# Merge gates of a hybrid decoder layer moved to the front and formed by seven half-size products

## The chip, the cores and the metric

One core of a Trainium2 chip runs the whole layer as one program. The metric is the device time of that core in microseconds. The engines in the text: PE is the tensor engine (its weight loads are PEld), DVE the vector engine, ACT the scalar engine, POOL is GpSimd, SP issues most transfers. A product is one matmul instruction with a 128x128 stationary part and 512 moving columns.

## The reference

One layer on 512 tokens with 2048 features, in float32:

```python
h = _rms_norm(x, norm_g[i])
proj = jnp.einsum("bld,dn->bln", h, w_in[i])
(z_ssd, xbc, dt, u_pool, z_pool, q, k, v, z_attn, gate_logits) = jnp.split(proj, IN_SPLITS, axis=-1)
y_ssd = _ssd_branch(z_ssd, xbc, dt, ...)
y_pool = _pool_branch(u_pool, z_pool, ...)
y_attn = _attn_branch(q, k, v, z_attn, ...)
gates = jax.nn.sigmoid(gate_logits.reshape(b, seq, N_BRANCHES, D_MODEL))
merged = (gates[:, :, 0] * (y_ssd @ w_br_ssd[i])
          + gates[:, :, 1] * (y_pool @ w_br_pool[i])
          + gates[:, :, 2] * (y_attn @ w_br_attn[i]))
x = x + merged @ w_out[i]
ple_gate = jax.nn.sigmoid(_rms_norm(x, ple_norm_g[i]) @ w_ple_gate[i])
x = x + ple_gate * (p[i] @ w_ple_proj[i])
```

The gate logits are h (512 x 2048) times 6144 columns of w_in, 2048 for each branch. y_ssd and y_pool have 2048 features, y_attn 512.

## The kernel before

Everything on PE is fed by one weight stream. `plan` lists entries of 512 KB; for each, `load` (L93) issues a transfer on SP into one of three `raw` buffers, and `split` (L101) makes two float32r parts of it: `hi` by a cast on ACT (L116), `lo` by a subtraction on DVE (L117; on POOL for entries 2 to 5). There are three `hi` and three `lo` buffers, so the cast of an entry waits until PE is through with the entry three before it. A job asks for the split two entries ahead of the one that it multiplies, and `split` asks for the load three further. Each pair of blocks takes three products: hi x hi, hi x lo, lo x hi (`product`, L124). So an entry has 24 products. `job_a` (L129) is token-major: 256 rows by 512 columns of weights move, the activations stand, and four PSUM banks fill at once. `job_b` (L157) is feature-major: the weights stand (512 rows by 256 columns), the tokens move, and two banks fill.

Activations are kept the same way: Hh and Hl are the two parts of the normed input, feature-major (128 features x 512 tokens, 16 of them). Small steps of the branches stand in two queues, `tasks` and `other`; `tick` (L74) runs one step of each after each entry, and `flush` runs them all. All four engines work in the order in which the program names their instructions. Short-lived tiles, 128x512, come from one pool `tp` of 52; transposes and small products use three PSUM banks (`PS`), the jobs five (`PG`).

The order of the jobs: the embedding's projection (kept in DRAM as ple_d, with the transposes of x beside it, `x_turn`), attention q, k, v, Z_ATT, SSD's dt and xbc, its z, then three merges. A merge (L910) alternates `gate_job`, whose two banks go through a sigmoid on ACT to SBUF (L894), with `br_job`, whose banks are multiplied by the gate on DVE (L903) and added to m on POOL (L907). Two gate jobs stand ahead of each first branch job, and m comes out feature-major, as the output projection needs it. `y_norm`, `ya_split` and `yp_split` make the branch's two parts as tasks beside these gate jobs, `m_split` those of m. The pooling jobs stand between the attention merge and the last; `pooled` (L953) runs beside its Z_POOL jobs.

Of the kernel before, what the change touches and what calls it, by code (L numbers as in the profile page):

```python
# [9 lines left out]
F32 = mybir.dt.float32  # L10
# [16 lines left out]
# groups 1 and 2 work on blocks of every 4th token (a block of group 2 holds 4 of its 16 strides)  # L27
# [4 lines left out]
def hybrid_kernel(ctx: ExitStack, tc: tile.TileContext, x, p, norm_g, w_in, conv_w, conv_b, dt_bias, a_log,  # L32
# [11 lines left out]
    tp = ctx.enter_context(tc.tile_pool(name="tp", bufs=NT))  # L44
    wp = ctx.enter_context(tc.tile_pool(name="wp", bufs=3))
    psum = ctx.enter_context(tc.tile_pool(name="psum", bufs=3, space=PSUM))
    dram = ctx.enter_context(tc.tile_pool(name="dram", bufs=1, space=DRAM))
    ctx.enter_context(tc.manual_schedule())

    def T(name="t", dtype=F32):  # L50
        return tp.tile([128, L], dtype, name=name, tag="t")
# [41 lines left out]
    def load(n):  # L93
        while state["dma"] <= n and state["dma"] < len(plan):
            src, k, c = plan[state["dma"]]
            t = wp.tile([128, k, c], F32, name="raw", tag="raw", bufs=3)
            nc.sync.dma_start(out=t, in_=src.rearrange("(k p) c -> p k c", p=128))
            raws[state["dma"]] = t
            state["dma"] += 1

    def split(n):  # L101
        while state["split"] <= n and state["split"] < len(plan):
            i = state["split"]
            load(i)
            r = raws.pop(i)
            _, k, c = plan[i]
            if c == 32:
                # the narrow entry keeps its two parts side by side
# [4 lines left out]
            else:  # L113
# [4 lines left out]
                parts[i] = (hi, lo)  # L118
            state["split"] += 1
# [9 lines left out]
    def job_a(w, c0, kn, xk, evac, pre=None, post=None):  # L129
        """Token-major [128 tokens, 512 columns]; xk(kt, t) gives the activations' two parts."""  # L130
# [26 lines left out]
    def job_b(w, c0, kn, xk, evac, pre=None, post=None, tiles=2):  # L157
        """Feature-major [128 features, 512 tokens]; xk(kt) gives the activations' two parts."""
# [46 lines left out]
    def rsqrt(dst, src, tmp, inv_n):  # L205
        """dst = 1 / sqrt(src * inv_n + EPS), with one Newton step behind the table."""
# [38 lines left out]
    def load_columns():  # L245
# [6 lines left out]
        # d_skip of the head that a feature belongs to  # L252
# [21 lines left out]
    def warm(n):  # L274
        """Products that nobody reads keep the tensor engine's clock up until the first weights are in."""
        ps = PG()
        for _ in range(n):
            PE.matmul(ps[:, 0:128], lhsT=ident, rhs=ident, start=True, stop=True)

    def start():  # L280
# [9 lines left out]
        def g_rows(j):  # L290
            # the selected row of norm_g on every partition
# [84 lines left out]
    hook(flush)  # L376
    hook(lambda: tasks.append(load_columns()))

# [4 lines left out]
    def make_masks():  # L383
# [3 lines left out]
        # keys of the block before: k >= q; of the same block: k <= q  # L387
# [6 lines left out]
        # every 16th token: within a block of every 4th, the keys whose place is the query's modulo 4  # L394
# [146 lines left out]
    zs_att, Ya = {}, {}  # L541

    def za_evac(j):
        def f(n, ps):
            z = T("za")
            A.activation(z, ps, AF.Silu)
            zs_att[2 * j + n] = z
# [4 lines left out]
    def combine():  # L552
# [34 lines left out]
        for h in range(4):  # L587
# [11 lines left out]
            V.tensor_mul(o, o, zs_att[h])  # L599
            Ya[h] = o  # L600

    for j in range(2):
        job_b(w_in, Z_ATT + j * 256, 16, hk, za_evac(j))

# [41 lines left out]
    def dt_task(o):  # L646
# [19 lines left out]
        # softplus(v) = max(v, 0) + log1p(e), e = exp(-|v|); log1p(e) = 2 atanh(e / (2 + e))  # L666
# [54 lines left out]
    def load_bc(n):  # L721
        """The rows of cumulated log decays of chunk n % 4 and the heads of group n // 4, on every partition."""
        while bc_at["n"] <= min(n, 15):
# [5 lines left out]
            if c > 0:  # L729
                # the growth since the chunk's start: even heads on partitions 0-63, odd ones on 64-127  # L730
# [155 lines left out]
    hook(lambda: tasks.append(y_norm()))  # L886

# [1 line left out]
    m, gs, done = {}, {}, {i: 0 for i in range(16)}  # L889

    def gate_job(br, f):
        def ev(n, ps):
            g = T("g")
            A.activation(g, ps, AF.Sigmoid)  # L894
            gs[2 * f + n] = g
        job_b(w_in, GATES + br * D + f * 256, 16, hk, ev)

    def br_job(w, kn, xk, f, first, pre=None):
        def ev(n, ps):
            i = 2 * f + n  # L900
            done[i] += 1
            g = gs.pop(i)
            V.tensor_mul(g, g, ps)  # L903
            if first:
                m[i] = g
            else:
                G.tensor_tensor(m[i], m[i], g, op=ALU.add)  # L907
        job_b(w, f * 256, kn, xk, ev, pre=pre)

    def merge(br, w, kn, xk, first, pre=None, after_gates=None):  # L910
        gate_job(br, 0)
        for f in range(8):
            if f < 7:
                gate_job(br, f + 1)
# [204 lines left out]
```

## Time and profile before

| what | us |
|---|---|
| median of the two runs | 2709.87 |
| the runs | 2712.01 and 2707.73 |
| span of the profiled execution | 2707.0 |
| median above that span | 2.9 |

The page counts busy time of each engine over the span and follows the chain of work that ended last. The profiled execution has no time of its own beside its span; the two runs lie 0.7 and 5.0 us above it. PE rows overlap: a product's row lasts about 0.39 us, while the next starts 0.23 us later, so the pitch is read from starts, not from durations. A row "out<-in" names the tile written and the tiles read; "[4.38 <-PE pg L126]" behind it is the idle time before it and what ended that.

### The profile page before, as it was taken

What the parts mean: (1) busy time and instruction counts of PE and PEld (TensorE: products, weight loads), DVE (VectorE), ACT (ScalarE), POOL (GpSimd) and SP (SyncE); (2) the same over time, 40 slices, a digit from 0 to 9 for tenths busy, and PEclk for the clock granted to TensorE, in tenths of its full rate; (3) what the DMA queues carried; (4) which work ended last, traced back from release to release, by engine and by line L of the source; (5) the groups of instructions that cost most, each with busy time, mean ns of one, the idle gap of its engine ahead of it and who ended that gap; (6) DMA issues with size and microseconds to landing.
All of it is one profiled execution on the core that took longest, in us unless ns stands there. A gap on an engine that the chain in (4) does not pass through costs nothing.

```text
span 2707.0 us, 29886 instructions
## 1 busy us (share of the span) xinstructions
PE 2689.0 (99%) x12310; PEld 2236.5 (83%) x12310; DVE 1098.3 (41%) x1456; ACT 840.0 (31%) x1133; POOL 208.7 (8%) x198
## 2 busy tenths in 40 slices
PE   8999999999999999999999999999999999999999
PEld 6888989888788888888888888888888888888887
DVE  6334333346776655322223333334442222433333
ACT  4233333443444434222222222222242222322322
POOL 5000000001211113000000110000000000000000
PEclk9999999999999999999999999999999999999999
DMA  7422323234644423333333333333333333333343
GB/s 227 100 88 77 94 78 94 77 93 105 168 118 127 113 86 86 109 94 101 94 101 93 101 94 98 97 94 101 87 108 93 101 94 97 113 114 119 112 153 101
DMA packets 238672, 284.56 MB, mean 105 GB/s; under 512 B 12620, under 2 KB 187528, under 8 KB 238536
## 3 DMA queue, kind: packets, MB, share of 16 engines
q1 hardware_dynamic: 236968, 278.74, 34.6%
q0 software_dynamic: 1568, 3.92, 1.0%
q8 instruction: 96, 1.57, 0.2%
q14 instruction: 40, 0.33, 0.0%
HBM read 274.08 MB, written 8.54 MB: 104 GB/s over the span
## 4 chain that ended last, share of the span: by engine, by line
PE 96%; DVE 2%; DMA 1%; ACT 1%; issue 0%; SPq 0%; DVEq 0%; ACTq 0%
PE pg L125 31%; PE pg L126 31%; PE pg L127 31%; PE ps L802 1%; PE ps L490 0%; PE ps L458 0%; PE ps L421 0%; DVE cv L614 0%; PE ps L785 0%; DVE x L326 0%; PE ps L791 0%; DVE ple L365 0%; PE ps L1044 0%; PE ps L477 0%; DVE lo L117 0%
## 5 line engine op out<-in xcount | busy, mean ns | idle before, releaser
L117 DVE TENSOR_TENSOR lo<-raw,hi 128x1024 fp32r<-128x1024 f32 x464 | 585.2, 1262 | 1221.7 <-ACT hi L116 1219.2
L116 ACT CAST hi<-raw 128x1024 fp32r<-128x1024 f32 x468 | 490.5, 1051 | 1153.7 <-PE pg L126 820.3
L125 PE MATMUL pg<-hh,hi 128*128 128x512 f32 x1984 | 782.7, 394 | 0.0
L127 PE MATMUL pg<-hh,lo 128*128 128x512 f32 x1984 | 772.5, 389 | 0.0
L126 PE MATMUL pg<-hl,hi 128*128 128x512 f32 x1984 | 772.4, 389 | 0.0
L125 PEld LDWEIGHTS pg<-hh,hi 128*128 128x128 f32 x1984 | 372.6, 188 | 81.2 <-issue 3.9
L126 PEld LDWEIGHTS pg<-hl,hi 128*128 128x128 f32 x1984 | 372.7, 188 | 78.4 <-issue 3.1
L127 PEld LDWEIGHTS pg<-hh,lo 128*128 128x128 f32 x1984 | 372.5, 188 | 78.0
L125 PE MATMUL pg<-hi,hh 128*128 128x512 f32 x576 | 230.0, 399 | 0.0
L127 PE MATMUL pg<-hi,hl 128*128 128x512 f32 x576 | 225.8, 392 | 0.0
L126 PE MATMUL pg<-lo,hh 128*128 128x512 f32 x576 | 225.7, 392 | 0.0
L127 PEld LDWEIGHTS pg<-hi,hl 128*128 128x128 f32 x576 | 124.2, 216 | 17.8
L125 PEld LDWEIGHTS pg<-hi,hh 128*128 128x128 f32 x576 | 124.4, 216 | 16.5
L126 PEld LDWEIGHTS pg<-lo,hh 128*128 128x128 f32 x576 | 124.4, 216 | 16.4
L907 POOL TENSOR_TENSOR g<-g 128x512 f32<-128x512 f32 x32 | 41.9, 1308 | 1216.7 <-DVE g L903 1192.3
L125 PE MATMUL pg<-hi,mh 128*128 128x512 f32 x256 | 100.1, 391 | 0.0
L125 PE MATMUL pg<-hi,xh 128*128 128x512 f32 x256 | 99.8, 390 | 0.0
L127 PE MATMUL pg<-hi,ml 128*128 128x512 f32 x256 | 99.7, 389 | 0.0
L126 PE MATMUL pg<-lo,mh 128*128 128x512 f32 x256 | 99.6, 389 | 0.0
L127 PE MATMUL pg<-hi,xl 128*128 128x512 f32 x256 | 99.6, 389 | 0.0
L126 PE MATMUL pg<-lo,xh 128*128 128x512 f32 x256 | 99.6, 389 | 0.0
L125 PE MATMUL pg<-yh,hi 128*128 128x512 f32 x256 | 99.6, 389 | 0.0
(289 smaller groups left out, 2722.2 us busy)
## 6 DMA issues: line engine op xcount, KB each, us to landing
raw<-in_w_in_dram SPq DMA_DIRECT2D x320, 512.0 KB, 3.6
raw<-in_w_br_ssd_dram SPq DMA_DIRECT2D x32, 512.0 KB, 3.5
raw<-in_w_br_pool_dram SPq DMA_DIRECT2D x32, 512.0 KB, 3.5
raw<-in_w_out_dram SPq DMA_DIRECT2D x32, 512.0 KB, 3.6
raw<-in_w_ple_gate_dram SPq DMA_DIRECT2D x32, 512.0 KB, 3.6
bc<-acT_d SPq DMA_DIRECT2D x32, 256.0 KB, 4.7
x<-in_x_dram SPq DMA_DIRECT2D x16, 256.0 KB, 6.8
ple_d<-ple SPq DMA_DIRECT2D x16, 256.0 KB, 2.8
```

The lines of the kernel that those rows point to most:

```text
L116: A.copy(hi, r)
L117: (G if 1 < i < EARLY else V).tensor_tensor(lo, r, hi.bitcast(F32), op=ALU.subtract)
L125: PE.matmul(ps, lhsT=lh, rhs=rh, start=first, stop=False)
L126: PE.matmul(ps, lhsT=lh, rhs=rl, start=False, stop=False)
L127: PE.matmul(ps, lhsT=ll, rhs=rh, start=False, stop=last)
L802: PE.matmul(pd[q, rows(h // 2)], lhsT=xdt[:, h * 64:h * 64 + 64], rhs=bc[h // 4][:, rows(h % 4)], start=True, stop=True)
L907: G.tensor_tensor(m[i], m[i], g, op=ALU.add)
```

## The change

The gates of all three branches are formed first, right after the embedding's projection, and stored in DRAM (gate_d). They are made in six blocks of 1024 columns by Strassen's method in Winograd's form: h is cut in two halves of tokens and two of features (L11, L12, L21, L22), the weights in two of rows and two of columns (a, b over c, d). Four sums S1 to S4 of h's quarters are made once (`make_left`), and four T1 to T4 of the weights' for each entry (T2 = d - b + a, T3 = d - b, T1 = d - T2, T4 = T2 - c). The seven products are L11 a, S2 T2, S3 T3 in a first pass, S4 d, S1 T1 in a second, L12 c, L22 T4 in a third; d is loaded twice. Each entry has 12 products. The results are summed on DVE in `st` tiles, go through a sigmoid on ACT and are stored by ACT's own transfers. While this runs, the pool of 52 tiles is closed and its room holds the sums (`swap`).

The branch products become token-major (`job_a`) and read their gates from DRAM, four tiles of 128x512 at a time; m is token-major and is turned by transposes (`m_turn`). The Z_ATT jobs move behind SSD's z, its result and the attention's go through DRAM (za_d, ya_d), and the attention merge moves into the first pooling group, behind its U_POOL jobs. `PS` has two banks, `PG` six. The cut diff:

```diff
-        return psum.tile([128, L], F32, name="ps", tag="s", bufs=3)
+        return psum.tile([128, L], F32, name="ps", tag="s", bufs=2)
-        return psum.tile([128, L], F32, name="pg", tag="g", bufs=5)
+        return psum.tile([128, L], F32, name="pg", tag="g", bufs=6)
...
     def split(n):
         while state["split"] <= n and state["split"] < len(plan):
             i = state["split"]
+            if callable(plan[i]) and "sp" not in held:
+                return
             load(i)
-            r = raws.pop(i)
-            _, k, c = plan[i]
+            if callable(plan[i]):
+                r, k, c = plan[i]("raw"), 2, L
...
+    def make_left():
...
+        for q0 in (0, 4):
+            x = {}
+            for n in ("L11", "L21", "L22", "L12"):
+                x[n] = sp.tile([128, 4, 256], F32, name="x4", tag="t2", bufs=4)
+                (G if n == "L12" else V).tensor_tensor(x[n], part(0, n), part(1, n), op=ALU.add)
+            x["S3"] = sp.tile([128, 4, 256], F32, name="x4", tag="rs", bufs=2)
+            V.tensor_sub(x["S3"], x["L11"], x["L21"])
+            V.tensor_add(x["L22"], x["L21"], x["L22"])
+            V.tensor_sub(x["L11"], x["L22"], x["L11"])
+            V.tensor_sub(x["L12"], x["L12"], x["L11"])
+            for n, o in (("S2", "L11"), ("S3", "S3"), ("S4", "L12"), ("S1", "L22")):
+                h, l = (SC[n][i][:, q0:q0 + 4] for i in range(2))
+                A.copy(h, x[o])
+                V.tensor_sub(l, x[o], h.bitcast(F32))
+            yield
...
+        passes.append([(entry("a", e, (("a", False),)), entry("T2", e, (("b", True), ("d", False))),
+                        entry("T3", e, ())) for e in range(4)])
+        passes.append([(entry("d", e, (("d", False),)), entry("T1", e, ())) for e in range(4)])
+        passes.append([(entry("c", e, (("c", False),)), entry("T4", e, ())) for e in range(4)])
+        lefts = (("L11", "S2", "S3"), ("S4", "S1"), ("L12", "L22"))
...
+                elif name == "S1":
+                    o = tile_()
+                    V.tensor_add(st["u2", t], st["u2", t], p)
+                    V.tensor_add(o, st["u3", t], p)
+                    evac(t, 1, st["u2", t], st["u2", t])
+                    evac(2 + t, 1, o, o)
+                elif name == "L12":
+                    evac(t, 0, p, tile_())
+                elif name == "L22":
+                    V.tensor_sub(st["u3", t], st["u3", t], p)
+                    evac(2 + t, 0, st["u3", t], st["u3", t])
...
+    def gate_evac(br, j):
+        def f(t, half, src, o):
+            A.activation(o, src, AF.Sigmoid)
+            c = (j + half) * L
+            nc.scalar.dma_start(out=gate_d[br, rows(t), c:c + L], in_=o)
+        return f
+
+    def enter():
+        swap("sp")
+        load(state["split"])
+        split(state["split"])
+        tasks.append(make_left())
+        step(tasks)
+
+    hook(enter)
+    for br in (0, 2, 1):
+        for j in (0, 2):
+            s_block(GATES + br * D + j * L, gate_evac(br, j))
+    hook(lambda: swap("tp"))
...
+        for j in range(4):
+            job_a(w, j * L, kn, lambda kt, t: tuple(a[:, rows(t)] for a in xk(kt)), ev(j),
+                  pre=lambda j=j: (pre() if pre and j == 0 else None, load_gates(br, j)),
+                  post=(lambda j=j: after(j)) if after else None)
...
+    def m_turn(j):
...
+        yield
+        for k in range(4):
+            kt = 4 * j + k
+            ps = PS()
+            for t in range(4):
+                PE.transpose(ps[:, rows(t)], m[t, j][:, rows(k)], ident)
+            A.copy(MT["h"][:, kt], ps)
+            V.tensor_sub(MT["l"][:, kt], ps, MT["h"][:, kt].bitcast(F32))
+            if k % 2:
+                yield
+
+    merge(1, w_br_pool, 16, lambda kt: Yph[kt], False, pre=flush, after=lambda j: tasks.append(m_turn(j)))
+    hook(lambda: [step(tasks) for _ in range(2)])
```

The instructions at three places. First DVE where the normed input is complete; hl is its second part, turned by `x_turn`. Before:

```order
L336 TENSOR_TENSOR hl_99<-pg_552,hh_98 128x4x128
L396 TENSOR_REDUCE mask_559<-ident_74 128x4
L397 TENSOR_SCALAR mask_559<-mask_559 128x4
L399 TENSOR_TENSOR mask_559<-mask_559 128x128
L117 TENSOR_TENSOR lo_580<-raw_351,hi_579 128x1024
```

After that, only the masks stand ahead of the next weight entry's lo.

The same place on DVE in the changed kernel; the x4 tiles are quarter sums of h, t2 is T2, rs holds b and then T3 (the last hl and two more L239 rows stand just ahead):

```order
L239 TENSOR_TENSOR x4_578<-hh_98,hl_99 128x1024
L241 TENSOR_TENSOR x4_582<-x4_574,x4_576 128x1024
L242 TENSOR_TENSOR x4_578<-x4_576,x4_578 128x1024
L243 TENSOR_TENSOR x4_574<-x4_578,x4_574 128x1024
L244 TENSOR_TENSOR x4_580<-x4_580,x4_574 128x1024
L248 TENSOR_TENSOR S2l_569<-x4_574,S2h_568 128x1024
L248 TENSOR_TENSOR S3l_571<-x4_582,S3h_570 128x1024
L248 TENSOR_TENSOR S4l_573<-x4_580,S4h_572 128x1024
L248 TENSOR_TENSOR S1l_567<-x4_578,S1h_566 128x1024
L274 TENSOR_TENSOR rs_560<-raw_562,rs_560 128x1024
L276 TENSOR_TENSOR t2_596<-rs_560,raw_554 128x1024
L137 TENSOR_TENSOR lo_607<-rs_560,hi_606 128x1024
```

The first half of `make_left`, eleven rows, has come in between hl and the first T2 and T3; its second half follows the last row shown, and the masks stand behind the gates.

Second, SP at the same place. Before:

```order
L97 DMA raw_447<-in_w_in_dram 128x2x512
L368 DMA ple_d_81<-ple_491 128x512
L368 DMA ple_d_81<-ple_494 128x512
L368 DMA ple_d_81<-ple_497 128x512
L368 DMA ple_d_81<-ple_500 128x512
L97 DMA raw_577<-in_w_in_dram 128x2x512
```

The last four stores of the embedding's projection are shown; a load of w_in stands ahead of each such four. In the changed kernel, from the last store but one:

```order
L536 DMA ple_d_81<-ple_488 128x512
L536 DMA ple_d_81<-ple_491 128x512
L264 DMA raw_554<-in_w_in_dram 128x2x512
L264 DMA rs_560<-in_w_in_dram 128x2x512
L264 DMA raw_562<-in_w_in_dram 128x2x512
L264 DMA raw_564<-in_w_in_dram 128x2x512
```

All sixteen stores now stand ahead of the first load of w_in.

Third, ACT where gates leave PSUM; hi is the cast of a weight entry. Before, at the start of the last merge:

```order
L116 CAST hi_13790<-raw_13686 128x1024
L894 ACTIVATE g_13820<-pg_13688 128x512
L894 ACTIVATE g_13822<-pg_13701 128x512
L116 CAST hi_13824<-raw_13730 128x1024
L116 CAST hi_13856<-raw_13764 128x1024
L116 CAST hi_13886<-raw_13794 128x1024
```

Two sigmoids stand between two casts, and eight casts follow before the next two. In the changed kernel, at the end of the first block's second pass (st is a sum of products, t2 a T4):

```order
L136 CAST hi_991<-t2_596 128x1024
L551 ACT_TABLE_LOAD
L551 ACTIVATE st_818<-st_818 128x512
L553 DMA gate_d_100<-st_818 128x512
L551 ACTIVATE st_1009<-st_1009 128x512
L553 DMA gate_d_100<-st_1009 128x512
L551 ACTIVATE st_820<-st_820 128x512
L553 DMA gate_d_100<-st_820 128x512
L551 ACTIVATE st_1016<-st_1016 128x512
L553 DMA gate_d_100<-st_1016 128x512
L136 CAST hi_1023<-raw_958 128x1024
L136 CAST hi_1040<-t2_666 128x1024
```

Four sigmoids and four stores stand between the cast of the first T4 and that of the second c.

More of the change, by code (lines that the diff above doesn't have):

```diff
@@ L94, in load @@
         while state["dma"] <= n and state["dma"] < len(plan):
[L95 to L98, printed above, removed]
+            if callable(plan[state["dma"]]):
+                if "sp" not in held:
+                    return
+                plan[state["dma"]]("load")
+            else:
+                src, k, c = plan[state["dma"]]
+                t = wp.tile([128, k, c], F32, name="raw", tag="raw", bufs=3)
+                nc.sync.dma_start(out=t, in_=src.rearrange("(k p) c -> p k c", p=128))
+                raws[state["dma"]] = t
             state["dma"] += 1
@@ L118, in split @@
                 parts[i] = (hi, lo)
+            if callable(plan[i]):
+                plan[i]("done")
             state["split"] += 1
@@ L185, in hook, with left, part @@
         jobs.append((f, lambda: None))
+    SC = {}
+    def left(name, kt, t):
+        c = slice(128 * t, 128 * t + 128)
+        if name[0] == "L":
+            q = slice(256 * (name[1] == "2") + 128 * t, 256 * (name[1] == "2") + 128 * t + 128)
+            kt += 8 * (name[2] == "2")
+            return HT[0][:, kt, q], HT[1][:, kt, q]
+        return SC[name][0][:, kt, c], SC[name][1][:, kt, c]
+    def make_left():
+        sp = held["sp"]
+        for n in ("S1", "S2", "S3", "S4"):
+            SC[n] = tuple(sp.tile([128, 8, 256], F32R, name=n + "hl"[i], tag=n + "hl"[i]) for i in range(2))
+        def part(i, name):
+            return HT[i][:, 8 * (name[2] == "2") + q0:8 * (name[2] == "2") + q0 + 4,
+                         256 * (name[1] == "2"):256 * (name[1] == "2") + 256].bitcast(F32)
+        for q0 in (0, 4):
[13 more added lines that the diff above has]
+            yield
@@ L539, in hybrid_kernel @@
         attention(gi)
-    zs_att, Ya = {}, {}
+    za_d = dram.tile([4, 128, L], F32, name="za_d")
+    ya_d = dram.tile([4, 128, L], F32, name="ya_d")
     def za_evac(j):
@@ L546, in f @@
             A.activation(z, ps, AF.Silu)
-            zs_att[2 * j + n] = z
+            nc.scalar.dma_start(out=za_d[2 * j + n], in_=z)
         return f
@@ L598, in combine @@
             V.tensor_add(o, o, oo[2, h])
[L599 to L603, printed above, removed]
+            G.dma_start(out=ya_d[h], in_=o)
     conv = {}
@@ L886, in hybrid_kernel, with load_gates, merge, ev @@
     hook(lambda: tasks.append(y_norm()))
[L889 to L914, printed above, removed]
-            if f == 6 and after_gates:
-                hook(after_gates)
-            br_job(w, kn, xk, f, first, pre=pre if f == 0 else None)
+    for j in range(2):
+        job_b(w_in, Z_ATT + j * 256, 16, hk, za_evac(j))
+    m, gs, MT = {}, {}, {}
+    def load_gates(br, j):
+        for t in range(4):
+            gs[t, j] = T("g")
+            nc.sync.dma_start(out=gs[t, j], in_=gate_d[br, rows(t), j * L:(j + 1) * L])
+    def merge(br, w, kn, xk, first, pre=None, after=None):
+        def ev(j):
+            def f(t, ps):
+                g = gs.pop((t, j))
+                V.tensor_mul(g, g, ps)
+                if first:
+                    m[t, j] = g
+                else:
+                    G.tensor_tensor(m[t, j], m[t, j], g, op=ALU.add)
+            return f
+        for j in range(4):
+            job_a(w, j * L, kn, lambda kt, t: tuple(a[:, rows(t)] for a in xk(kt)), ev(j),
+                  pre=lambda j=j: (pre() if pre and j == 0 else None, load_gates(br, j)),
+                  post=(lambda j=j: after(j)) if after else None)
     merge(0, w_br_ssd, 16, lambda kt: (Yh[kt], Yl[kt]), True, pre=flush)
@@ L924, in ya_split, with merge_att @@
         for h in range(4):
+            y, z = T("ya"), T("za")
+            nc.sync.dma_start(out=y, in_=ya_d[h])
+            nc.sync.dma_start(out=z, in_=za_d[h])
+            Yah[h] = (y, z)
+        yield
+        yield
+        for h in range(4):
+            y, z = Yah[h]
+            V.tensor_mul(y, y, z)
             a, b = T("yah", F32R), T("yal", F32R)
-            split_to(a, b, Ya[h])
+            split_to(a, b, y)
             Yah[h] = (a, b)
             yield
+    def merge_att():
+        merge(2, w_br_attn, 4, lambda kt: Yah[kt], False, pre=flush)
     hook(lambda: tasks.append(ya_split()))
-    merge(2, w_br_attn, 4, lambda kt: Yah[kt], False, pre=flush)
     inv = const.tile([128, 16], F32, name="inv")
@@ L988, in pool_group @@
                   post=(lambda: tasks.append(pooled())) if i else None)
+        if g == 0:
+            merge_att()
         for i in range(2):
```

113 lines of the change are left out of this document (99 added, 14 removed).

## The prediction

> **What bounds the kernel now.** I read the share of busy time first, then the chain of work that ended last, then busy time by 50 us stretches (columns: PE, PEld, DVE, ACT, POOL busy with counts, granted clock, DMA share, GB/s), then single rows.
>
> ```profile
> PE 2689.0 (99%) x12310; PEld 2236.5 (83%) x12310; DVE 1098.3 (41%) x1456; ACT 840.0 (31%) x1133; POOL 208.7 (8%) x198
> PE 96%; DVE 2%; DMA 1%; ACT 1%; issue 0%; SPq 0%; DVEq 0%; ACTq 0%
> 0.00:50.00 50.00, 39.17 (x174) 29.77 (x175) 34.06 (x64) 27.62 (x64) 29.33 (x31) 0.99 0.79 274
> 1150.00:1200.00 50.00, 50.00 (x222) 41.40 (x222) 13.39 (x12) 10.57 (x11) 0.00 (x0) 1.00 0.31 95
> ...
> 2600.00:2650.00 50.00, 50.00 (x222) 41.44 (x221) 16.12 (x18) 12.05 (x13) 2.17 (x4) 1.00 0.41 137
> ```
>
> These five rows say one thing: after the first 50 us the tensor engine never waits long, and 96% of the last chain is its own work. The first of the two late stretches runs gates and branch products feature-major, the second runs token-major products; both hold 222 products, so the layout of a product is free. The pitch of a product comes from the casts of one weight entry, which follow the entries:
>
> ```profile
> 1148.67 1.05 ACT L116 CAST hi<-raw 128x1024 fp32r<-128x1024 f32 x1 [4.38 <-PE pg L126]
> ...
> 1164.99 1.05 ACT L116 CAST hi<-raw 128x1024 fp32r<-128x1024 f32 x1 [4.38 <-PE pg L126]
> ```
>
> These are four casts, three entries apart: 16.32 / 3 = 5.44 us for 24 products, 0.2267 us each. ACT is idle 4.38 us in each entry, and DVE is busy 13.4 of 50 us in that stretch. That idle time is what the change spends.
>
> **Products removed and transposes added.** The gates are 24 jobs of 96 products, 2304 in all. Seven half-size products give each of the six blocks 28 entries of 12, 2016 in all. 288 fewer x 0.2267 = **-65.3 us**, all on the path. Turning m costs 16 groups of four transposes.
>
> ```profile
> 2394.62 0.87 PE ps L1044 x8
> PE ps L802 <- DVE bc L781: 1.2, 2, 0.8
> ```
>
> Eight transposes take 0.87 us in the chain of waits, so 64 take **+7.0 us**, on the path too, since the engine has no idle time. The sums m, g*ps and the sigmoids keep their numbers.
>
> **The start.** Before, the products resume at 51.3 because their first weights had been cast long before. Rows of that place, with the durations that the new work will have:
>
> ```profile
> 42.85 5.23 SPq L368 DMA_DIRECT2D ple_d<-ple  x4
> 48.39 2.45 PE L332 MATMUL ps<-ident,x 128*128 128x128 f32 x12 [4.49 <-DVE hl L336]
> 50.63 1.06 PE L332 MATMUL pg<-ident,x 128*128 128x128 f32 x4
> 51.34 0.78 PE L125 MATMUL pg<-hi,hh 128*128 128x512 f32 x1
> 51.91 0.63 PE L126 MATMUL pg<-lo,hh 128*128 128x512 f32 x1
> 52.34 0.51 PE L127 MATMUL pg<-hi,hl 128*128 128x512 f32 x1
> 52.68 0.40 PE L125 MATMUL pg<-hi,hh 128*128 128x512 f32 x1
> ...
> 52.34 0.69 DVE L336 TENSOR_TENSOR hl<-pg,hh 128x512 fp32r<-128x512 f32 x1 [0.16 <-ACT hh L335]
> ...
> 56.08 1.22 DVE L117 TENSOR_TENSOR lo<-raw,hi 128x1024 fp32r<-128x1024 f32 x1
> ...
> L117 POOL TENSOR_TENSOR lo<-raw,hi 128x1024 fp32r<-128x1024 f32 x4 | 9.6, 2402 | 4.2 <-ACT hi L116 4.2
> raw<-in_w_in_dram SPq DMA_DIRECT2D x320, 512.0 KB, 3.6
> ```
>
> Now no gate weight may be loaded until the last ple_d store is issued (48.1). Block a lands 3.6 later, is cast after the last hh (52.3 to 53.4), and its lo is still one of the early ones on POOL, 2.40 long: 55.8. The entry has 2.7 us of products and ends at 58.4, which loses 4.3 against 51.4. From 53.0 DVE makes the first halves of the sums of h: 11 operations of 1.23 are 13.5 us, to 66.5. Behind them in its queue stand the two that make T2 (2.5), then come the cast (1.05) and a lo on POOL (2.4): 72.5. The T2 entry ends at 74.8, having waited 13.6. T3 runs to 77.5. DVE meanwhile has the second halves, 13.5 us and about 1 us for POOL's sum, from 72.3 to 87, ahead of the lo of the next a: that entry waits 10.1. The next T2 waits 2.1 more. The sum is **+30 us**; I bound it by 26 (POOL's lo and DVE's overlap better) and 35. The exit from the gates has the same form, the masks on DVE behind the last gate stores, but there two entries lie cast ahead, 10.9 us, and I cost it at nothing; if the stores land 3 us later than I think, it shows.
>
> Two banks instead of three for the transposes make x_turn's third group wait for DVE to empty the first, once in each of the four token tiles: a transpose group, a cast and a subtraction are late by 0.7 to 1 us each, **+3 us** (0 to 5).
>
> The clock: in the rows above, after 4.49 us without work, 16 transposes take 3.0 us where 1.7 is usual, and the first three products start 0.57, 0.43 and 0.34 apart. That is about 2 us lost for one pause, so two long pauses cost **+4 us** (0 to 5). [...]
>
> **Inside the six blocks.** An entry now holds 12 products, 2.72 us. Each still needs a cast and a lo.
>
> ```profile
> L117 DVE TENSOR_TENSOR lo<-raw,hi 128x1024 fp32r<-128x1024 f32 x464 | 585.2, 1262 | 1221.7 <-ACT hi L116 1219.2
> L116 ACT CAST hi<-raw 128x1024 fp32r<-128x1024 f32 x468 | 490.5, 1051 | 1153.7 <-PE pg L126 820.3 <-PE pg L127 290.1 <-issue 28.6
> L903 DVE TENSOR_TENSOR g<-g,pg 128x512 f32<-128x512 f32 x48 | 33.0, 688 | 59.1 <-PE pg L127 59.1
> L894 ACT ACTIVATE g<-pg 128x512 f32<-128x512 f32 x48 | 28.5, 598 | 87.5 <-PE pg L127 87.5
> ...
> 2528.85 0.38 SPq L97 DMA_DIRECT2D raw<-in_w_ple_gate_dram  x1
> ```
>
> In the first pass a step (a, T2, T3) gives DVE five operations, 6.3 us in 8.16 us of products: it keeps up, with about 1 us to spare in the chain subtract, add, cast, lo of T2, because an hi buffer comes free only when the entry three back is done. In the other passes DVE has 3.8 in 5.44. So inside a pass nothing waits. At the ends of passes it does. Count from the start of c's first entry, when the S1 products have just ended. DVE still holds the lo of the first T4, to 2.0; then come the adds of 0.69. Each of four gates then takes on ACT a sigmoid (0.60), a hand-over and the issue of its store, for which the nearest row is SP's issue (0.38): 1.1 us each, 2.7 to 7.1. The cast of the second c stands behind them: 8.2, its lo 9.4. It was due at 5.44 and a product later, so the tensor engine waits 3.9 us, and 0.9 more at the T4 after. At the end of the third pass four gates again stand ahead of a cast: 1.9 and 0.6. At the end of the first, S1's bank comes free 0.4 late. That is 7.6 us for a block (5.1 for the first, whose predecessor is missing): **+43 us**. If the issue on ACT cost 0.1, a block would lose 5.7, 34 in all; with hand-overs of 0.1 us everywhere 9.5, 57 in all. ACT's issue is not in the trace of before; 0.38 is taken because SP's is the same kind of transfer.
>
> **Covers lost.** Before, two gate jobs ran ahead of each branch; y_norm gets the Z_ATT jobs in their place, the others get nothing.
>
> ```profile
> L982 DVE SCALAR_TENSOR_TENSOR zp<-pg,cols,zp 128x512 f32<-128x512 f32 x16 | 12.0, 750 | 18.3 <-PE pg L127 18.3
> L217 DVE TENSOR_TENSOR ypl<-zp,yph 128x512 fp32r<-128x512 f32 x16 | 10.1, 685 | 4.5 <-ACT yph L216 4.5
> L964 DVE SCALAR_TENSOR_TENSOR q<-s,u 128x512 f32<-128x512 f32 x16 | 11.1, 692 | 0.6
> L907 POOL TENSOR_TENSOR g<-g 128x512 f32<-128x512 f32 x32 | 41.9, 1308 | 1216.7 <-DVE g L903 1192.3 <-issue 23.2 <-ACT hi L116 1.1
> ```
>
> The first pool product waits for a last evacuation (0.75) and one ypl (0.69): 1.2. The pooled() chain of group 0 is flushed ahead of the attention merge's splits; four features of some 3.2 us (four or five such rows each) are 13 us against two entries of cover, 10.9: 2.5. The last turn of m waits for 0.69 on DVE and 1.31 on POOL, then its third and fourth groups for a bank: 3.7. Together **+7.4** (4 to 10). The gate loads (48 of 256 KB) stand on SP behind weights already issued five entries ahead and are needed eight entries later: nothing. Two banks in attention and SSD: the only wait of PE there is the L802 row above, 1.2 us; DVE is the later one anyway, so **+3** (0 to 8). The za and ya round trip is eight stores and eight loads with whole jobs between: nothing.
>
> **Sum.** -65.3 + 7.0 + 30 + 3 + 4 + 43 + 7.4 + 3 = +32 on the span of 2707.0: 2739. The median of the runs, 2709.87, lies 2.9 above that span, so 2742. With each term at its lower bound the sum is +6 (26, 0, 0, 34, 4, 0 for the six estimates in the order of their parts, start first), 2716; with each at its upper bound +62 (35, 5, 5, 57, 10, 8), 2772.
>
> **Rivals.** A: the ends of passes are covered. ACT might issue for almost nothing and the tasks might drain sooner. Against it stands the order on ACT, four stores ahead of a cast. It gives the sum with 43 replaced by nothing, about 2699. B: transfers bind the first pass. It loads three entries of 512 KB in 8.16 us, and decides once a load takes more than 2.72. One load alone takes 3.6 to land in the row above; if they landed one after another, a step would take 10.8, and 24 steps x 2.64 = 63 us more: 2805, slower by 3.5%. Against it: the first 50 us moved 274 GB/s at a share of 0.79, where this needs 193. C: the change does what its count of products says, with no new wait but the transposes: 2652. It would need DVE to make 22 operations at the start in no time; the rows exclude most of it.
>
> **Numbers.** Forecast 0.70, with its own range 2716 to 2772; A 0.13; B 0.14; C 0.03. The range 2698 to 2772 leaves out B and C, 0.17. 2% is 54 us, about what a measurement of this kernel can tell from no change: faster by over 2% (below 2656) is C, 0.03; slower by over 2% (above 2764) is B and the top of the forecast, 0.06, so 0.20; within it 0.77.
>
> **What would show it.** In the changed trace: 2016 products in the gates at 0.227; two pauses of PE over 8 us between 58 and 95 us, released by DVE and POOL; six waits of 3 to 5 us, one in each block, released by a lo behind a cast whose ACT queue held gate stores; 64 transposes at 0.11. It is wrong if those six waits are under 2 us (then A), or if PE waits for raw or rs within a first pass (then B), or if the start costs under 20 us.

## The result and the profile after

| | us |
|---|---|
| before, median of 2 runs | 2709.87 |
| after, median of 2 runs (2755.87 and 2756.26) | 2756.07 |
| ratio, with its 95% interval | 1.0169 (1.0139 to 1.0198) |
| span of the profiled execution after | 2753.4 |

The kernel is 46 us slower, 1.7%. Forecast were 2742 and a change within 2%, too small to be told. The interval leaves out 1, so the change can be told. The page after, busy time and the shares of the chain that ended last:

```profile
PE 2668.3 (97%) x12086; PEld 2203.5 (80%) x12086; DVE 1351.7 (49%) x1718; ACT 926.1 (34%) x1223; POOL 223.8 (8%) x204
PE 86%; DVE 7%; ACT 4%; issue 2%; ACTq 0%; DMA 0%; POOL 0%; SPq 0%; DVEq 0%
```

PE has 224 instructions fewer (288 products out, 64 transposes in), but the chain now runs through DVE and ACT for 11% of the span, where it was 3%. DVE has 253 us more work. The stretches of 50 us show where (columns: PE, PEld, DVE, ACT, POOL busy, granted clock, DMA share, GB/s):

```profile
50.00:100.00 50.00, 20.15 (x67) 14.49 (x68) 43.74 (x38) 15.01 (x19) 12.94 (x5) 0.68 0.34 101
100.00:150.00 50.00, 49.83 (x216) 40.78 (x215) 37.69 (x37) 21.44 (x23) 0.00 (x0) 0.98 0.44 125
...
2600.00:2650.00 50.00, 50.00 (x222) 41.41 (x221) 16.20 (x17) 13.86 (x15) 2.21 (x4) 1.00 0.44 140
```

From 50 to 100 us PE works for 20 of 50 us at a clock of 0.68 while DVE is 87% busy: that is the start of the gates. The waits of PE, in total, times, longest:

```profile
PE pg L348 <- ACT hi L136: 34.8, 9, 12.7
PE pg L348 <- DVE lo L137: 11.4, 18, 1.9
PE ps L500 <- DVE hl L504: 10.3, 5, 4.7
...
PE ps L990 <- DVE eb L976: 3.7, 1, 3.7
PE ps L681 <- ACT et L671: 2.7, 1, 2.7
```

L348 is the gates' product, L500 the transposes of x, L681 the product of the transposed scores `et` with v in attention, and L990 products of SSD that wait until DVE has read a PS bank into `eb`. No row names `raw` or `rs` as what a gate product waits for.

Where the difference of the two spans (46.4) lies, by the starts of the first products of each part. A job moved from one part to another is taken out at 96 x 0.2267 = 21.76 us:

| part | before | after | difference |
|---|---|---|---|
| up to the first product after x is turned | 51.3 | 57.4 | +6.1 |
| the gates (24 jobs; six blocks) | 522.3 | 533.8 | +11.5 |
| attention, SSD, Z_ATT | 988.6 | 999.8 | +11.2 |
| the three merges and the pooling | 783.3 | 800.0 | +16.7 |
| output projection and the rest | 361.5 | 362.4 | +0.9 |

The gates' 2016 products are worth 457.0 us, so they lost 76.8 us: 31.7 up to 97.5 us, and 45.1 in the blocks. Of the 16.7 in the merges 6.4 are the 64 transposes (by the starts 0.80 for each eight that stand without a wait).

### The profile page after: what moved, and what is told of

Its sections match the earlier page's. It is cut to its first block, busy times and chain, and to the rows that moved or that the text cites. A ratio compares the mean times of both kernels' runs of the same rounds, so it can differ in the third digit from the quotient of the medians.

```text
span 2753.4 us, 30122 instructions
## 1 busy us (share of the span) xinstructions
PE 2668.3 (97%) x12086; PEld 2203.5 (80%) x12086; DVE 1351.7 (49%) x1718; ACT 926.1 (34%) x1223; POOL 223.8 (8%) x204
## 4 chain that ended last, share of the span: by engine, by line
PE 86%; DVE 7%; ACT 4%; issue 2%; ACTq 0%; DMA 0%; POOL 0%; SPq 0%; DVEq 0%
PE pg L147 24%; PE pg L148 24%; PE pg L149 24%; PE pg L348 10%; ACT hi L136 2%; DVE lo L137 2%; ACT st L551 1%; PE ps L990 1%; PE ps L681 0%; DVE t L276 0%; DVE cv L802 0%; DVE rs L274 0%; PE ps L649 0%; DVE x L239 0%; ACTq L553 0%
## 5 line engine op out<-in xcount | busy, mean ns | idle before, releaser
L147 PE MATMUL pg<-hh,hi 128*128 128x512 f32 x1216 | 485.0, 399 | 0.0
L148 PE MATMUL pg<-hl,hi 128*128 128x512 f32 x1216 | 474.5, 390 | 0.0
L149 PE MATMUL pg<-hh,lo 128*128 128x512 f32 x1216 | 474.3, 390 | 0.0
L147 PEld LDWEIGHTS pg<-hh,hi 128*128 128x128 f32 x1216 | 229.0, 188 | 51.6 <-issue 4.8
L148 PEld LDWEIGHTS pg<-hl,hi 128*128 128x128 f32 x1216 | 229.0, 188 | 48.8 <-issue 3.1
L149 PEld LDWEIGHTS pg<-hh,lo 128*128 128x128 f32 x1216 | 228.8, 188 | 48.3
L147 PE MATMUL pg<-hi,hh 128*128 128x512 f32 x576 | 229.6, 399 | 0.0
L149 PE MATMUL pg<-hi,hl 128*128 128x512 f32 x576 | 225.6, 392 | 0.0
L148 PE MATMUL pg<-lo,hh 128*128 128x512 f32 x576 | 225.5, 391 | 0.0
L348 PE MATMUL pg<-hi,hh 128*128 128x512 f32 x288 | 118.3, 411 | 22.1 <-ACT hi L136 22.1
L348 PE MATMUL pg<-lo,hh 128*128 128x512 f32 x288 | 118.4, 411 | 9.4 <-DVE lo L137 6.7
L348 PE MATMUL pg<-hi,hl 128*128 128x512 f32 x288 | 116.7, 405 | 0.0
L136 ACT CAST hi<-t 128x1024 fp32r<-128x1024 f32 x48 | 50.4, 1050 | 151.4 <-DVE t L276 82.8
L147 PE MATMUL pg<-hi,yph 128*128 128x512 f32 x256 | 100.1, 391 | 0.0
```

The lines of the kernel that those rows point to most:

```text
L136: A.copy(hi, r)
L147: PE.matmul(ps, lhsT=lh, rhs=rh, start=first, stop=False)
L148: PE.matmul(ps, lhsT=lh, rhs=rl, start=False, stop=False)
L149: PE.matmul(ps, lhsT=ll, rhs=rh, start=False, stop=last)
L348: PE.matmul(ps[name][t], lhsT=lh, rhs=r[:, k], start=first and i == 0, stop=last and i == 2, skip_group_check=name in ("L11", "L12"))
```

## The experiments

**The ends of the blocks.** In the second block, the sigmoids and stores on ACT (ACTq issues the stores), and PE behind them:

```profile
231.56 0.63 ACT L551 ACTIVATE st<-st 128x512 f32<-128x512 f32 x1 [1.89 <-DVE st L324]
232.22 0.33 ACTq L553 DMA_DIRECT2D gate_d<-st  x1
232.59 0.63 ACT L551 ACTIVATE st<-st 128x512 f32<-128x512 f32 x1 [0.40 <-ACT st L551]
...
235.80 1.04 ACT L136 CAST hi<-raw 128x1024 fp32r<-128x1024 f32 x1 [0.45 <-ACT st L551]
236.90 0.49 PE L348 MATMUL pg<-hi,hh 128*128 128x512 f32 x1 [2.24 <-ACT hi L136]
238.16 0.50 PE L348 MATMUL pg<-lo,hh 128*128 128x512 f32 x1 [0.77 <-DVE lo L137]
```

Each gate takes ACT 1.03 us from start to start: 0.63 of sigmoid and 0.40 of store and hand-over. The cast of the second c comes at 235.80, and PE waits 2.24 for it and 0.77 for its lo. The same pair of waits stands in every block, 83.7 us apart (from 154.03 in the first to 572.40 in the sixth: 418.37 / 5), where a block's 336 products make 76.2.

First the stores alone were taken off ACT:

```diff
-            nc.scalar.dma_start(out=gate_d[br, rows(t), c:c + L], in_=o)
+            nc.gpsimd.dma_start(out=gate_d[br, rows(t), c:c + L], in_=o)
```

> The changed kernel, with each gate store issued from POOL's queue in place of ACT's; the sigmoids stay where they are. Theory 1 (at the end of a block PE waits for the cast of c_1, which stands on ACT behind four sigmoids of 0.63 us and four store issues of 0.33 us): the cast comes 4 x 0.33 = 1.3 us earlier at each second c and about as much at the end of the third pass, so a block loses about 5.5 to 6 us in place of 7.5 and the time falls by 8 to 13 us, to 2743 to 2748. Rival (what holds PE there is DVE's chain of sums, subtractions and lo's, or the arrival of c, and ACT only happens to be the last): the waits keep their length, within 3 us of the changed kernel. Second rival: an issue on POOL is dear or late and holds the tiles of the gates; then the waits move to T3_0 of the next block and the time rises by up to 5 us.

Measured 2732.96 (2731.89 to 2733.91), 23 us less, twice what was expected. At the same place:

```profile
228.80 2.43 ACT L551 ACTIVATE st<-st 128x512 f32<-128x512 f32 x4 [1.89 <-DVE st L324]
231.13 1.03 ACT L136 CAST hi<-raw 128x1024 fp32r<-128x1024 f32 x1
232.21 0.50 PE L348 MATMUL pg<-hi,hh 128*128 128x512 f32 x1 [0.31 <-ACT hi L136]
```

Four sigmoids in a row now take 2.43 us, 0.60 each, so the store had cost its issue (0.33) and some 0.1 besides. The wait is 0.31 in place of 2.24, the later one at T3_0 (1.0) is gone, and a block takes 80.1 us. The clock is the rest: after the waits of the changed kernel it fell, here it did not (5 us each, the changed kernel's third block, then this one's):

```profile
320.00:325.00 5.00, 4.02 (x9) 2.84 (x10) 3.34 (x3) 2.45 (x3) 0.00 (x0) 0.55 0.29 71
```
```profile
310.00:315.00 5.00, 3.93 (x16) 2.72 (x16) 3.05 (x4) 2.50 (x5) 2.02 (x4) 1.00 0.58 210
```

Then sigmoid and store were made a step of the queue, one after each entry, on ACT as before:

```diff
-        def f(t, half, src, o):
+        def one(t, half, src, o):
...
+            yield
+        def f(t, half, src, o):
+            other.append(one(t, half, src, o))
...
-    hook(lambda: swap("tp"))
+    hook(lambda: (flush(), swap("tp")))
```

> The changed kernel, with each gate's sigmoid and its store made a step of the queue of other work, one at the end of each product step, in place of four in a row; that queue is emptied before the pools are swapped back. Theory 1 (the four sigmoids and stores in a row ahead of a cast on ACT are what PE waits for): at each tick ACT then has one sigmoid and one issue (0.96 us) beside a cast of about 0.7 us, which fits in a step of 2.7 us; the wait at the second c (3.4 us) and at T3_0 (1.0 us) go, the halved clock behind them too (1.7 us), and a block loses 1.5 to 3 us in place of 7.5: 27 to 36 us less in all, 2720 to 2729. Rival (DVE's chain or the loads bind there): within 5 us of the changed kernel, the waits being put down to DVE. Between the two, 10 to 20 us less, would mean that DVE is next in line a little behind ACT.

Measured 2724.40 (2722.74 to 2725.54), 31.7 us less, as theory 1 has it. A block takes 78.3 us. One wait of some size is left in it, at the second T4:

```profile
235.28 0.50 PE L348 MATMUL pg<-lo,hh 128*128 128x512 f32 x1 [0.50 <-DVE lo L137]
```

So DVE, which makes each T4 and its lo, is next in line, but half a microsecond behind. The order of the work on ACT was the cause, not the amount: ACT's busy time is 923.0 against 926.1. What is left, 2.1 us in a block by the starts, is small waits; those that the list names are for DVE.

**What the seven products are worth.** The gates as twelve ordinary `job_a` of 512 columns, first and into DRAM as before, without blocks, sums or swap:

```diff
-    hook(enter)
...
-            s_block(GATES + br * D + j * L, gate_evac(br, j))
-    hook(lambda: swap("tp"))
+        for j in range(4):
+            job_a(w_in, GATES + br * D + j * L, 16, hkt, plain_evac(br, j))
```

> The changed kernel, with the gates still first and in DRAM, but as twelve ordinary jobs of 16 row tiles by 512 columns (2304 products in place of 2016), with no half-size blocks, no sums of h and no swap of pools; the merges by tokens, the transposes of m and the PS and PG banks stay. Theory 1 (the seven products pay 65.3 us and cost 31.7 at the start and 45.1 at the block ends, so they are worth minus 11 net, and the rest of the loss, 35 us, is the reorganisation): 2740 to 2749. Rival (ordinary jobs pay much the same at their ends, since each of the twelve also ends with four sigmoids and stores on ACT): each end then costs 3 to 4 us, 12 times, and the time is 2775 to 2795. Second rival: even without waits the reorganisation costs less than counted, below 2735.

Measured 2739.69 (2737.69 to 2743.51): with 288 products more the kernel is 16 us faster. Its profile has no wait in the gates. So the seven products as built are worth less than nothing, and 31 us of the loss have nothing to do with them.

**The PSUM banks.** The kernel before, with two PS and six PG banks (`bufs=3` and `5` made `2` and `6`):

> The kernel before, with two PS banks and six PG banks in place of three and five, and nothing else: the one part of the change that touches the prologue, the attention, the SSD part and the norms. Theory 1 (the two banks are what costs the changed kernel 6.1 us in the prologue and 11.2 us between the dt job and the first merge): 10 to 18 us slower than before, 2720 to 2728, with new waits at the states product and at the two attention jobs, released by ACT's or DVE's reading of a PS bank. Rival (x_turn takes three PS banks in a row in both, so the prologue's loss is the banks', but the other is due to the order, the Z job and gate 0 no longer standing where they did): 4 to 7 us slower. Second rival: no bank matters, within 2 us.

Measured 2720.44 (2719.52 to 2721.07), ratio 1.0042 (1.0027 to 1.0057): 11.4 us. By the starts 6.9 of them lie ahead of the attention's first q, where PE waits for the emptying of a PS bank 11.2 us in place of 4.5, and 4.4 in attention and SSD:

```profile
PE ps L332 <- DVE hl L336: 11.2, 4, 5.3
...
PE ps L802 <- DVE eb L788: 1.9, 1, 1.9
PE ps L559 <- ACT st L565: 1.6, 1, 1.6
```

The other way round, plain gates with three PS and five PG banks:

> The kernel with plain gates (2739.7 us), with three PS and five PG banks as in the kernel before in place of two and six. Theory 1 (of its 31 us over the kernel before, the banks cost what they cost the kernel before when it had two: 11 us): 2726 to 2731, with the four DVE waits of the prologue's transposes and the eb wait of the SSD part gone, while the wait of 2.7 us at the last attention block's et product and the waits at the merges stay, since these come from work that stood beside them before and no longer does. Rival (the banks and the order are one cause, and all waits between the gates and the first merge go with the third bank): 2718 to 2724. Second rival: five PG banks hold up the jobs of 16 row tiles by 512 columns: not below 2736.

Measured 2731.29 (2729.13 to 2736.61), 8.4 us less than with two (11.0 between the profiled spans). The prologue gets its 7.6 us back (first gate product at 50.4 in place of 58.0), attention and SSD only 3.1: the wait of 3.5 us for eb went, but two for a cast on ACT, 2.9 in all, came at the same line. The wait at the last attention block stays as it was, with the third bank there:

```profile
PE ps L500 <- DVE hl L504: 4.4, 1, 4.4
...
PE ps L679 <- ACT et L669: 2.7, 1, 2.7
```

**The covers.** In the kernel before, Z_ATT's two jobs stood behind the attention. The change moves them behind SSD's z, beside `y_norm`. Here they go back, the U jobs of pool group 0 stand beside `y_norm`, and its Z jobs ahead of the attention merge; that merge and the first wait only for their own task, not for all:

```diff
+    for j in range(2):
+        job_b(w_in, Z_ATT + j * 256, 16, hk, za_evac(j))
     hook(dt_prep)
...
     hook(lambda: tasks.append(y_norm()))
-    for j in range(2):
-        job_b(w_in, Z_ATT + j * 256, 16, hk, za_evac(j))
+    for i in range(2):
+        job_b(w_in, U_POOL + i * 256, 16, hk, u_evac(i))
```

> The changed kernel with the covers in another order and nothing else: the two Z_ATT jobs stand directly behind the attention, as in the kernel before, the U jobs of pool group 0 beside the norm of y, and the Z jobs of group 0 ahead of the attention merge. Theory 1 (the changed kernel lost 4 to 5 us at the last attention block, since Z_ATT was its cover, and some 4 us at the merges for the same reason): the wait of 2.7 us at the et product and the halved clock behind it go, the waits for yah and its lo go, 6 to 9 us less in all, 2747 to 2750. Rival (the two PS banks hold the last attention block, with or without cover): that wait stays, 2751 to 2754. Second rival: the U jobs cover the norm less well, and the gain is given back at the first merge: 2755 or more.

Measured 2746.88 (2743.98 to 2748.64), 9.2 us less, with two banks still. Attention, SSD and Z_ATT, by the same starts, take 990.7 us: 9.1 less than in the changed kernel and some 2 more than in the kernel before. The merges are 3.9 shorter. The wait at the et product is gone from the list, and so are the two of 0.8 at the products with yah in the attention merge (these were for the hi and the lo of a weight entry). The one for eb, 3.7 us before, is 0.2:

```profile
PE ps L993 <- DVE eb L979: 0.2, 1, 0.2
```

So most of the 11.2 us there came from the lost cover. But two banks cost the kernel before 4.4 in the same stretch, and a third bank gave 3.1 back without the cover: the stretch answers to both, and the eb wait, 3.7 us in the changed kernel and 0.2 here, was 2.1 in both kernels that only changed the gates' stores. How the 11.2 divide was not settled.

**The start.** Rows of DVE, then of POOL, in the changed kernel:

```profile
57.18 7.81 DVE L239 TENSOR_TENSOR x<-hh,hl 128x1024 f32<-128x1024 f32 x3
64.91 1.21 DVE L241 TENSOR_TENSOR x<-x,x 128x1024 f32<-128x1024 f32 x1
...
81.29 3.48 DVE L239 TENSOR_TENSOR x<-hh,hl 128x1024 f32<-128x1024 f32 x3
```
```profile
57.45 3.14 POOL L137 TENSOR_TENSOR lo<-raw,hi 128x1024 fp32r<-128x1024 f32 x1 [6.71 <-ACT hi L136]
60.55 3.35 POOL L239 TENSOR_TENSOR x<-hh,hl 128x1024 f32<-128x1024 f32 x1
```

Three sums of L239 take 7.81 us the first time (1.21, 3.36 and 3.39 one by one) and 3.48 the second, when POOL is idle. To see whether POOL is the reason, its early lo's were given to DVE (`EARLY = 6` made `2`):

> The changed kernel, with the four early subtractions of lo (POOL, 2.4 to 3.1 us each) on DVE, so that POOL has only the two sums of L12 beside DVE at the start of the gates. Theory 1 (DVE and POOL slow each other while both read and write SBUF: the three sums of the first half took 2.6 us each while POOL worked and 1.2 us each alone): a sum of DVE that runs while POOL is idle takes 1.2 us, one beside POOL's sum of L12 2 to 2.6 us, and the lo of a_0 and T2_0 take about 1.2 us on DVE; the start is 0 to 5 us shorter. Rival (the sums are slow for another reason, such as the first reading of h behind the prologue's writes): the three sums stay at 2.6 us whatever POOL does, and the time is up by 2 to 4 us for the lo's that DVE now also has.

One run: 2749.81. POOL's sum of L12 now ends before DVE's sums begin, and they take 3.48 us (DVE, then POOL):

```profile
55.86 2.02 DVE L137 TENSOR_TENSOR lo<-raw,hi 128x1024 fp32r<-128x1024 f32 x1
57.80 3.48 DVE L239 TENSOR_TENSOR x<-hh,hl 128x1024 f32<-128x1024 f32 x3
```
```profile
54.43 2.36 POOL L239 TENSOR_TENSOR x<-hh,hl 128x1024 f32<-128x1024 f32 x1 [3.98 <-ACT hh L503]
```

That is theory 1 for the sums, from one run: the second a's first lo product starts at 92.7 us for 97.5, and 2.8 of that are left at the attention's first q. (The lo on DVE overlaps POOL's sum and takes 2.02, not 1.2.) The larger part of the start should then be that nothing covers DVE. So the two Z_ATT jobs were put ahead of the first block, and `make_left` cut into eight steps beside them, on top of the deferred stores, with the covers of the last experiment for the merges:

```diff
     def enter():
         swap("sp")
-        load(state["split"])
-        split(state["split"])
         tasks.append(make_left())
-        step(tasks)
...
     hook(enter)
+    for j in range(2):
+        job_b(w_in, Z_ATT + j * 256, 16, hk, za_evac(j))
+    hook(flush)
```

> The kernel with deferred gate stores (2724.4 us), with the two Z_ATT jobs in front of the first block and the sums of h cut into eight steps beside them, in place of all of one half's sums in a row; the U jobs of pool group 0 take Z_ATT's place beside the norm of y, and the Z jobs of group 0 stand ahead of the attention merge. No work is left out. Theory 1 (the start's 31.7 us are DVE's 22 sums and lo's with no products beside them): 43.5 us of products of Z_ATT cover about 27 us of DVE work there; the first block begins without a wait over 2 us; the merges' waits for yah and lo go (1.6 us): 2692 to 2702, below the kernel before. Rival (the sums are held by more than the want of cover, such as the clock or the loads of b and d): the start still costs 10 us or more, 2705 to 2715. Second rival: the U jobs cover the norm of y less well than Z_ATT did, and the gain is given back at the first merge.

Measured 2693.03 (2689.67 to 2695.55), ratio to before 0.9939 (0.9926 to 0.9953): faster than the kernel before, and 31.4 us faster than without the cover. In the same stretch as above DVE is busy as long (42.4 us) and PE more than twice as much:

```profile
50.00:100.00 50.00, 46.69 (x204) 38.56 (x205) 42.37 (x38) 20.02 (x23) 11.18 (x5) 0.93 0.39 119
```

The way to the attention is 28.1 us shorter with the two jobs taken out, and 3.7 came from the merges; attention and SSD changed by 0.4. The cover and the eight steps were put in together, so what each is worth alone is not shown. The et wait of 2.7 us is still there, since Z_ATT covers the start now and not the attention.

Three small things on top: the third of the four transposes of a token tile takes a PG bank, so does SSD's state product, and the dt job stands behind the first XBC job.

```diff
-            ps = PG() if j == 3 else PS()
+            ps = PG() if j >= 2 else PS()
...
-                po = PS()
+                po = PG()
...
+    job_b(w_in, XBC + 16 * 128, 16, hk, conv_evac(16))
     dt_job_entry = len(plan)
```

> The kernel with cover at the start, with three small things more: the prologue's transposes take PG banks for two of four tiles, the SSD part's state product takes a PG bank, and the dt job stands behind the first XBC job. Theory 1 (banks at the prologue 6 us, at the SSD part 4 us; 4 us at the last attention block for the cover that Z_ATT no longer gives, which an XBC job gives in its place): 10 to 14 us less than the kernel with cover alone, 2680 to 2690, about 1% below the kernel before. Rival (a PG bank taken by the transposes or by the state product holds up a job's own banks): less than 5 us less.

Measured 2687.27 (2682.34 to 2689.39), 5.8 us less, half of what was expected. The prologue gave its 6.3 us. The dt job's new place took the wait at the et product away, but a wait of 2.6 us took its place, at the transposes that combine the groups (L759), and SSD's wait stayed in spite of the PG bank (L998, another releaser):

```profile
PE ps L998 <- ACT hi L136: 3.6, 1, 3.6
...
PE ps L759 <- ACT st L765: 2.6, 1, 2.6
```

With a second XBC job ahead of dt (`for ct in (16, 18)`):

> The kernel with all parts (2687.3 us), with the dt job behind the second XBC job in place of the first. Theory 1 (one XBC job, 21.8 us, covers the last attention block but not the combining of the three groups behind it, where a wait of 2.6 us for an ACT copy has appeared; two jobs, 43.5 us, cover both as Z_ATT did): that wait goes, 3 to 5 us less, 2682 to 2685. Rival (the dt values come so late that the SSD part waits for them): a wait at the SSD part's first products of 5 us or more, 2690 to 2700.

Measured 2684.58 (2681.78 to 2684.95), 2.7 us less, but the runs of the two overlap. The 2.6 us wait went, smaller ones came (1.7 at L684, three at L759 of 1.6 in all), and attention and SSD together did not get shorter (by the starts 953.5, before this step 953.8). Nothing is settled by this pair.

Last, the turn of m's last quarter, made beside the first output job in place of ahead of it:

```diff
-    hook(lambda: [step(tasks) for _ in range(2)])
```

> The kernel with the dt job behind two XBC jobs (2684.6 us), with the turn of the last quarter of m no longer made ahead of the first output job but beside its first two entries; that job needs this quarter in its seventh entry. Theory 1 (the last turn of m lies bare on the path: two waits for POOL's sums of 0.9 us, one for a bank of 1.0 us, and a halved clock of 1.7 us behind them): all of it goes, 3 to 5 us less, 2680 to 2682, and the profile has no wait at the transposes of m over 0.3 us. Rival (the waits only move into the first output job, behind whose entries the transposes then stand in PE's order): within 1.5 us.

Measured 2679.33 (2676.85 to 2681.83), 5.2 us less; the longest of these runs and the shortest of the kernel before it (2681.78) just touch. What speaks for theory 1 is the trace: no wait at the transposes of m is left in the list, and the part from the first merge to the end is 5.1 us shorter by the starts. (The two profiled spans are equal, 2679.6, since those two runs were the profiled ones.) Its page:

```profile
PE 2646.4 (99%) x12086; PEld 2189.5 (82%) x12086; DVE 1350.6 (50%) x1718; ACT 925.2 (35%) x1226; POOL 222.7 (8%) x204
```

The same products as the changed kernel, with 22 us less of PE's busy time and 74 us less span. It beats both: 0.9890 of before (0.9872 to 0.9907).

## Why the prediction was right, and where it was not

The time lies in the stated range and within the 2%, 14 us above the 2742. But 2% was not the limit of what can be told: the interval of this ratio is 0.3% to either side. The sum was +32, measured were +46.4 between the spans. By its own steps:

- **Products removed, -65.3; transposes, +7.0.** Held: with plain gates the 2304 products ran without a wait, so the 288 are worth their pitch. The transposes take 6.4.
- **The start, +30, and the clock, +4.** 31.7 together. The order of events was as worked out: waits of 1.7 and 2.6, 12.7 and 1.6, 6.8 and 1.9, though the second long pause was to be over 8 and is that only with the lo behind it. The experiment with the cover, which removes 28.1, shows the cause, DVE's sums in a row with no products beside them.

```profile
57.42 0.59 PE L348 MATMUL pg<-hi,hh 128*128 128x512 f32 x1 [1.67 <-ACT hi L136]
60.64 0.79 PE L348 MATMUL pg<-lo,hh 128*128 128x512 f32 x1 [2.63 <-POOL lo L137]
...
77.91 0.80 PE L348 MATMUL pg<-hi,S2h 128*128 128x512 f32 x1 [12.70 <-ACT hi L136]
80.34 0.80 PE L348 MATMUL pg<-lo,S2h 128*128 128x512 f32 x1 [1.63 <-POOL lo L137]
...
94.81 0.79 PE L348 MATMUL pg<-hi,hh 128*128 128x512 f32 x1 [6.78 <-ACT hi L136]
97.52 0.79 PE L348 MATMUL pg<-lo,hh 128*128 128x512 f32 x1 [1.91 <-DVE lo L137]
```

- **The six blocks, +43.** 45.1, and 7.5 for a block where 7.6 stood, but by two errors that cancel. The waits named are there, each a little shorter: by the starts 3.4 at the second c for 3.9, 0.7 at T4 for 0.9, 1.0 at the end of the third pass for 2.5, 0.2 for 0.4; 5.3 in all. The other 2.2 are mostly the clock, for which the sum had nothing there. The mechanism, casts behind gates on ACT, is shown by both experiments on it.
- **The clock behind these waits.** The sum has the clock at the start alone, from one row, and nothing for it in the blocks. The granted clock fell to 0.50 after the second c in five of the six blocks, for 3.41 us in four of them and 6.83 in the third; over the stretches of 5 us there the missing clock adds up to 10.2 us, not all of it under products. The waits in front of it were 2.2 and 0.8 with a product between. The length of a wait does not settle it: the wait of 2.65 us at the et product is followed by a clock of 0.70 in the changed kernel and by 1.00 with plain gates, where it is 2.66 long.

```profile
1065.00:1070.00 5.00, 4.81 (x19) 4.28 (x20) 4.11 (x13) 3.31 (x6) 0.00 (x0) 0.70 0.27 65
```
```profile
1055.00:1060.00 5.00, 5.00 (x27) 4.25 (x28) 4.37 (x12) 3.64 (x5) 0.00 (x0) 1.00 0.31 83
```

The clock records show when. In the trace of the changed kernel the 13 halvings ahead of the last 6 us all start on one grid of 3.413 us (within 0.004) and last one to five of its steps, and they go with how far PE's rows fill the step just before. In this trace and that of the kernel before, without the first 20 us and the last 6 of each, all 12 steps at full clock that were less than 0.40 full were followed by a halving, none over 0.54 was, and of the four between two were (0.48 and 0.53 were, 0.46 and 0.49 were not). The wait at et fell into one step (1.34 us of PE's rows in 3.41, 0.39 full); with plain gates the grid of that trace, laid through its halving from 53.9 to 60.7 us, cuts it in two (0.47 and 0.75). In the changed kernel the grid also cut the waits of the first block, 2.2 and 0.8, which halved nothing (0.58 and 0.55).

- **Two banks in the prologue, +3 (0 to 5).** 6.1, twice the size and above the bound. The mechanism is right: two banks cost the kernel before 6.9 there, and a PG bank in their place gave 6.3 back.
- **Two banks in attention and SSD, +3 (0 to 8).** 11.2, above the bound, the largest miss and the step that failed. What the banks cost alone, 4.4 in the kernel before, lies within the bound. The prediction says that y_norm "gets the Z_ATT jobs in their place" and asks what the first merge loses; it does not ask what the attention loses, which had these jobs as cover for its last block. Put back, they remove 9.1 of it with two banks still; how the rest comes about stays open.
- **Covers lost at the merges, +7.4.** 10.3, a little above its bound of 10. The waits named were there (1.0 for ypl, 0.8 and 0.8 for a weight's hi and lo at the attention merge, 2.8 at the last turn of m), smaller than said, and twice the clock fell to 0.50 behind them, for 3.41 us each (at 1822.4 and 2389.0).
- **Rivals.** A (ends covered) fell by the six waits, which were 3.0 us each where under 2 was its mark; B (transfers) by the want of any wait for `raw` or `rs` in a gate product. C fell with both. But a covered end of the passes can be had, as A has it: deferring sigmoids and stores took 31.7 of its 43.
- **Its arithmetic.** Small slips, together under 3 us: the lo at 9.4 is 3.7 behind 5.67, where 3.9 stands; the terms of a block add up to 7.7, not 7.6; 12.8 us of `pooled` against 10.9 of cover are 1.9, not 2.5.

## What to carry to other kernels

A job that is moved takes its cover along: list what ran beside it at its old place as well as what it hides at the new one. On an engine that feeds the bound one, ask what small work stands in a row ahead of a cast, and whether it can be spread over the steps: here a block lost 7.5 us with four sigmoids and stores in a row and 2.1 with one after each entry, so their order alone was worth 32 us. And ask of a saving of products whether the engine that pays for it has other products beside it: here 65 us saved cost 77, of which the order on ACT and the cover at the start gave 60 back.

## What the runs showed of the hardware

- By their times DVE and POOL took turns in these sums. At 57 us three sums of DVE, 3.48 us alone, and two operations of POOL, 2.36 alone, took 7.81 us together, close to the sum of all five (8.2). One by one DVE's took 1.21, 3.36 and 3.39, POOL's 3.14 and 3.35: the first as long as alone, each later one its own time and about what the other still needed.
- A pause of PE cost clock here by how it lay on a grid of 3.413 us and not by its length alone: in the traces of the two kernels, their ends left out, each of the 12 steps at full clock that were less than 0.40 full was followed by a clock of 0.50, and none over 0.54 full.
- Behind a store that ACT issues, the next sigmoid starts 1.03 us after the last one in place of 0.60, though the issue itself is 0.33. POOL's issues of the same stores took 0.54 each (2.16 for four from 390 to 395 us), 26 us for the 48, and the kernel was 23 us faster than with the stores on ACT.
